# HGRN intra-chunk scores: one 128-column matmul against four 32-column matmuls, gathered in a compact tile

## The chip, the cores and the metric

The kernel runs on one core of a Trainium2 chip. The metric is the device time of one execution in microseconds (us); the time of a version is the median of several executions. The profile is of one further execution, taken by the hardware profiler.

## What is computed

The reference is one layer of a streaming encoder for 256 tokens of width 2048: a half SwiGLU block, a mixer with two recurrent branches, a cross attention, a second half SwiGLU block and a final norm. All weights are float32. The change touches only one branch of the mixer, the HGRN2 recurrence. Per head (8 heads, 128 key features, 128 value features) it is

```
S_t = diag(f_t) S_{t-1} + (1 - f_t) outer v_t,   o_t = S_t^T q_t
```

The reference works in chunks. The part that matters here is the score of a query token t against an earlier key token s, each feature decayed by the product of the forget gates between them:

```python
k = 1.0 - f
rel = b[:, :, :, None, :] - b[:, :, None, :, :]        # b: running sum of log f
decay = jnp.where(tri, jnp.exp(jnp.minimum(rel, 0.0)), 0.0)
scores = jnp.einsum('bhtk,bhsk,bhtsk->bhts', qc, kc, decay)
o_intra = jnp.einsum('bhts,bhsv->bhtv', scores, vc)
```

## The kernel before, in words

**The bulk of the kernel** is streamed weight products. A weight tile of 128x2048 float32 is fetched by a DMA on SP's queue, split by ScalarE (ACT, L120) into a high part in the reduced format fp32r and by VectorE (DVE, L121) into the rest, and multiplied by TensorE (PE) in three terms (`three` L446 to L452, `product` L224 to L245, `rows_product` L247 to L255). `weights` (L165) keeps two tiles prepared ahead of the one in use.

**The middle part** is a list of *units* (L876 to L901). A unit is one weight tile's product with the handling of its result: f, q, v, g for the HGRN branch in two halves of four heads, then the inputs of the other branch, then the gates. Beside them runs a list of *side jobs*, Python generators: `hgrn(0)`, `hgrn(1)`, `lru(0)`, `lru(1)`, `branch_a`. After each unit that does not return True, `pump(2)` (L658) advances the first side job by two steps; a step that ends in `yield True` ends the pump at once. `tc.issue_after(done["product"])` (L661) places what a side step issues on PE behind the unit's product. The framework orders the instructions of every engine at build time by their place in the program and its own model of when operands are ready; each engine then runs its list strictly in order.

**The HGRN job** (`hgrn`, L737 to L828) makes the score matrix of the 128 tokens of each of 2 groups x 4 heads, eight matrices in one SBUF tile `S` (128 partitions = key token, three times 512 columns; the third part holds the scores between the two groups). It works over levels n = 1, 2, 4, 8, 16, 32, 64 (`LEVELS`, L24): at level n a block of 2n tokens takes the scores of its second half's queries against its first half's keys, with q and k already decayed up to the block's middle. Ahead of the levels comes the diagonal (token against itself).

- Diagonal (L745 to L752): eight float32 matmuls with 128 key tokens as weight columns and 128 query tokens as moving columns, in two PSUM banks; DVE multiplies each bank by the identity into `S`.
- Levels 1 to 16 (L771 to L784): eight matmuls with 128 weight columns and the 64 queries that are in second halves; DVE multiplies the bank by a mask of 64 columns into a tile `part` (128x512), and in the next step adds `part` into the second halves' columns of `S`.
- Levels 32 and 64 (L759 to L770): for each block a matmul of its own, with n weight columns and n moving columns, placed at the block's partitions of the bank; ACT copies the blocks to `S` (L768).
- After each level DVE multiplies q and k by the block totals (L788), and makes the next totals (L793).
- The matrices then multiply the values (L807, L808), the result is normed and gated.

A float32 matmul stands in the trace as two records on PE and two weight loads on PEld.

`t1` (L90) hands out tiles of 128x256 float32 from a pool of eight, which the units use for the steps between accumulator and result (`summed`, L261).

Of the kernel before, what the change touches and what calls it, by code (L numbers as in the profile page):

```python
# [8 lines left out]
F32 = mybir.dt.float32  # L9
F32R = mybir.dt.float32r  # L10
ACT = mybir.ActivationFunctionType
ALU = mybir.AluOpType

P = 128
# [9 lines left out]
LEVELS = [1, 2, 4, 8, 16, 32, 64]  # L24
# [5 lines left out]
for _name, _n in [  # L30
    ("ffn1_norm", 16), ("mix_norm", 16), ("xattn_norm", 16), ("mem_norm", 16),
    ("ffn2_norm", 16), ("hgrn_norm", 8), ("lb0", 8), ("lb1", 8), ("lam", 8), ("conv_w", 32),
    ("conv_b", 8), ("ba", 8), ("bx", 8),
    ("ident", P), ("masks", 64 * 5),
]:
    VEC[_name] = (_at, _n)
    _at += _n
# [24 lines left out]
def block_kernel(ctx: ExitStack, tc: tile.TileContext, xT, xin, memT, vec, gfin, bgate, lruw, wu1, wd1, win, wv,  # L62
                 wg, wab, wout, wq, wk, wvm, wo, wu2, wd2, out_):
    nc = tc.nc
    pe, dve, act, sp = nc.tensor, nc.vector, nc.scalar, nc.sync
# [11 lines left out]
    scoped = {}  # L77
# [9 lines left out]
    def slot(dt=F32, name="slot"):  # L87
        return slots.tile([P, 1024], dt, name=name, tag="slot")

    def t1(name="t1"):  # L90
        return scoped["tmp"].tile([P, T], F32, name=name, tag="t1")

    def bank(name="acc"):
        return psum.tile([P, 512], F32, name=name, tag="acc")
# [6 lines left out]
    def col(name, i=0, n=1):  # L101
        a = VEC[name][0] + i
        return vt[:, a:a + n]
# [10 lines left out]
    ident = col("ident", 0, P)  # L114
# [551 lines left out]
    def heads(t):  # L666
        return t.rearrange("p (h t) -> p h t", h=4)
# [65 lines left out]


    Y = {}

    def hgrn(hf):  # L737
        q, f = Q[hf], F[hf]
        kk = slot(name="k")
        dve.tensor_scalar(out=kk, in0=f, scalar1=-1.0, scalar2=1.0, op0=ALU.mult, op1=ALU.add)  # L740
        yield True
        S = scoped["scores"].tile([P, 3 * 512], F32, name="S", tag="S")
        Sv = S.rearrange("p (g h t) -> p g h t", g=3, h=4)
        qv, kv = heads(q), heads(kk)
        for g in range(2):  # L745
            acc = bank()
            for h in range(4):
                pe.matmul(acc[:, h * P:(h + 1) * P], kv[:, h, g * P:(g + 1) * P], qv[:, h, g * P:(g + 1) * P],
                          start=True, stop=True)
            dve.tensor_tensor(out=Sv[:, g], in0=acc.rearrange("p (h t) -> p h t", h=4),  # L750
                              in1=ident[:, None, :].broadcast_to([P, 4, P]), op=ALU.mult)
            yield  # L752
        dve.tensor_tensor(out=q, in0=q, in1=f, op=ALU.mult)
        yield True
        tots = slot(name="tots")
        tot, at = f, 0
        for li, n in enumerate(LEVELS):
            acc = bank()
            if n >= 32:  # L759
                for g in range(2):  # L760
                    for h in range(4):
                        i = g * 4 + h
                        for a in range(0, P, 2 * n):
                            s = g * P + a
                            pe.matmul(acc[a:a + n, i * n:(i + 1) * n], kv[:, h, s:s + n], qv[:, h, s + n:s + 2 * n],
                                      start=True, stop=True)
                for a in range(0, P, 2 * n):
                    act.activation(S[a:a + n, :1024].rearrange("p (i t) -> p i t", t=P)[:, :, a + n:a + 2 * n],  # L768
                                   acc[a:a + n, :8 * n].rearrange("p (i n) -> p i n", n=n), ACT.Copy)
                yield  # L770
            for g in range(2 if n < 32 else 0):  # L771
                for h in range(4):
                    i = g * 4 + h
                    r = qv[:, h, g * P:(g + 1) * P].rearrange("p (j two n) -> p j two n", two=2, n=n)[:, :, 1]
                    pe.matmul(acc[:, i * 64:(i + 1) * 64], kv[:, h, g * P:(g + 1) * P], r, start=True, stop=True)  # L775
            if n < 32:
                part = scoped["tmp2"].tile([P, 512], F32, name="part", tag="part")
                dve.tensor_tensor(out=part.rearrange("p (i t) -> p i t", i=8),
                                  in0=acc.rearrange("p (i t) -> p i t", i=8),
                                  in1=col("masks", li * 64, 64)[:, None, :].broadcast_to([P, 8, 64]), op=ALU.mult)  # L780
                yield
                to = S[:, :1024].rearrange("p (i two n) -> p i two n", two=2, n=n)[:, :, 1]
                dve.tensor_tensor(out=to, in0=to, in1=part.rearrange("p (i n) -> p i n", n=n), op=ALU.add)
                yield  # L784
            pairs = tot.rearrange("p (j two) -> p j two", two=2)
            for t, side_of, by in ((q, 1, 0), (kk, 0, 1)):
                o = t.rearrange("p (j two n) -> p j two n", two=2, n=n)[:, :, side_of]
                dve.tensor_tensor(out=o, in0=o, in1=pairs[:, :, by:by + 1].broadcast_to([P, 512 // n, n]), op=ALU.mult)  # L788
                yield by == 1
            if n < 64:  # L790
                new = tots[:, at:at + 512 // n]
                at += 512 // n
                dve.tensor_tensor(out=new, in0=pairs[:, :, 0], in1=pairs[:, :, 1], op=ALU.mult)  # L793
                tot = new
        acc = bank()
        for h in range(4):
            pe.matmul(acc[:, h * P:(h + 1) * P], kv[:, h, :P], qv[:, h, P:], start=True, stop=True)
        act.activation(S[:, 1024:], acc, ACT.Copy)
        yield True
        y = Y["a", hf] = slot(name="ya")  # L800
        for pair in range(2):
            os, squares = [], []
            for z in range(2):
                h = pair * 2 + z
                c = (hf * 4 + h) * P
                o = bank()
                pe.matmul(o[:, :T], v[0][:, c:c + P], Sv[:, ::2, h, :], start=True, stop=False)  # L807
                pe.matmul(o[:, P:T], v[1][:, c:c + P], Sv[:, 1, h, :], start=False, stop=True)  # L808
                os.append(o)
                s = t1("osq")  # L810
                act.activation(s, o[:, :T], ACT.Square)
                squares.append(s)
            yield True
            ss = bank()
            for z in range(2):
                pe.matmul(ss[:, z * T:(z + 1) * T], ones, squares[z], start=True, stop=True)
            std = scoped["tmp2"].tile([P, 512], F32, name="ostd", tag="part")
            act.activation(std, ss, ACT.Sqrt, bias=eps, scale=1.0 / P)
            yield
            for z in range(2):  # L820
                h = pair * 2 + z
                o = heads(y)[:, h]
                r = std[:, z * T:(z + 1) * T]
                dve.reciprocal(out=r, in_=r)
                dve.tensor_tensor(out=o, in0=os[z][:, :T], in1=r, op=ALU.mult)
                dve.scalar_tensor_tensor(out=o, in0=o, scalar=col("hgrn_norm", hf * 4 + h), in1=heads(G[hf])[:, h],
                                         op0=ALU.mult, op1=ALU.mult)
                yield  # L828


    def lru(hf):
# [38 lines left out]
        yield  # L870
        y = Y["b", hf] = slot(name="yb")
        act.activation(GB[hf], GB[hf], ACT.Gelu_apprx_tanh)
# [20 lines left out]
    def branch_a():  # L893
        for h in range(8):
            ys.add(heads(Y["a", h // 4])[:, h % 4])
            yield
# [7 lines left out]
    for h in range(8):  # L904
        ys.add(heads(Y["b", h // 4])[:, h % 4])
    merged = Operands()
# [47 lines left out]
    for m in range(KT):  # L954
        acc = product(xs3.tiles, weights("q", m), late)
# [12 lines left out]
    for m in range(KT):  # L968
        acc = product(ms.tiles, weights("k", m))
# [38 lines left out]
    for g in range(4):  # L1008
# [4 lines left out]
        for t in range(2):  # L1013
            s = slot(F32R, "vs")
# [8 lines left out]
    for h in range(HEADS):  # L1023
        for j in range(4):
            acc = bank()
            for t in range(2):
                ps = probs[h][:, t * 512:(t + 1) * 512]
                s = vs[h, t]
# [50 lines left out]
def _layout(inputs):  # L1079
    import numpy as np  # L1080

    a = {k: np.asarray(v) for k, v in inputs.items()}
# [31 lines left out]
    def put(name, t):  # L1114
        at, n = VEC[name]
        vec[:, at:at + n] = t
# [6 lines left out]
    put("bx", vector(a["lru_bx"][0]))  # L1123
    put("lam", vector(a["lru_lambda"][0]))
    put("ident", np.eye(P, dtype=np.float32))
    s, t = np.arange(P)[:, None], np.arange(64)[None, :]
    put("masks", np.concatenate([(s // n == 2 * (t // n)) for n in LEVELS[:5]], axis=1).astype(np.float32))

    w = a["w_in"][0]
    win = columns(np.concatenate([w[:, :2048], w[:, 3072:6144]], axis=1))  # L1130
# [38 lines left out]
```

## Time and profile before

| what | value |
|---|---|
| median of 3 executions | 2468.77 us (2468.11 to 2469.32) |
| the profiled execution, its own time | 2467.42 us |
| its span in the profile | 2465.3 us |
| PE busy | 2446.9 us, 99% of the span |
| DVE busy | 1896.5 us, 77% |
| ACT busy | 1393.1 us, 57% |
| HGRN job of the first half of the heads | from 810.9 us to 949 us |
| HGRN job of the second half | from 937.8 us to 1088 us |
| diagonal matmuls, records on PE | 32 (16 matmuls) |
| level 1 to 16 matmuls, records on PE | 160 (80 matmuls) |
| granted TensorE clock | 0.999 |

Busy time is time in which an engine had at least one instruction in flight. A PE record's duration is longer than the interval at which PE starts records, since matmuls are pipelined; what a group of matmuls costs is read from the intervals between starts. The chain of waits is the work that ended last, followed back from the end of the execution; the length of a piece in it is the time it holds the end back.

### The profile page before, as it was taken

How to read it: one execution, taken by the hardware profiler on the slowest of the kernel's cores; microseconds unless marked ns; L12 is line 12 of the kernel's file. 1: busy time of each engine (PE TensorE's matmuls, PEld its weight loads, DVE VectorE, ACT ScalarE, POOL GpSimd, SP SyncE). 2: the span in 40 equal slices, each digit the busy share in tenths (PEclk: the TensorE clock that was granted, in tenths of full speed). 3: DMA queues.
4: the chain of work that ended last, by engine and by line, in shares of the span. 5: the costliest groups of instructions: out<-in, count | busy, mean ns of one | idle time of the engine just before them, and what ended most of it. 6: DMA issues, size and time to landing. Idle time of an engine off the chain costs nothing.

```text
span 2465.3 us, 29124 instructions
## 1 busy us (share of the span) xinstructions
PE 2446.9 (99%) x11674; PEld 2044.5 (83%) x11674; DVE 1896.5 (77%) x2016; ACT 1393.1 (57%) x1387; POOL 28.1 (1%) x36
## 2 busy tenths in 40 slices
PE   9999999999999999999999999999999999999998
PEld 7787888888888888888888888888888788888887
DVE  7989999999865757567665676556689899999995
ACT  8566666666564444358434554455555566666664
POOL 0000000000000000000000000000000000000000
PEclk9999999999999999999999999999999999999999
DMA  7567777777755455554655565554555777777774
GB/s 292 191 219 228 239 237 236 234 233 236 237 176 194 163 171 176 170 185 174 216 182 194 196 208 184 175 172 157 182 196 177 234 239 239 238 234 235 234 238 153
DMA packets 75303, 509.71 MB, mean 207 GB/s; under 512 B 8352, under 2 KB 8608, under 8 KB 15264
## 3 DMA queue, kind: packets, MB, share of 16 engines
q1 hardware_dynamic: 69840, 473.17, 56.0%
q0 software_dynamic: 4608, 33.56, 6.6%
q8 instruction: 91, 1.49, 0.2%
q10 hardware_dynamic: 720, 1.13, 0.1%
q14 instruction: 44, 0.36, 0.0%
HBM read 472.17 MB, written 2.10 MB: 192 GB/s over the span
## 4 chain that ended last, share of the span: by engine, by line
PE 92%; DVE 3%; ACT 2%; DMA 2%; issue 1%; SPq 0%; ACTq 0%; DVEq 0%
PE acc L452 16%; PE acc L449 16%; PE acc L450 16%; PE acc L231 11%; PE acc L252 8%; PE acc L253 8%; PE acc L255 8%; PE acc L235 5%; ACT h L120 1%; DMA raw<-wu 1%; DVE l L121 1%; PE acc L775 1%; PE acc L488 1%; PE acc L389 1%; DMA l<-raw 0%
## 5 line engine op out<-in xcount | busy, mean ns | idle before, releaser
L121 DVE TENSOR_TENSOR l<-raw,h 128x2048 fp32r<-128x2048 f32 (+2 forms) x420 | 874.8, 2085 | 334.7 <-ACT h L120 331.2
L120 ACT ACTIVATE h<-raw 128x2048 fp32r<-128x2048 f32 (+2 forms) x420 | 734.6, 1752 | 557.8 <-PE acc L253 227.1
L449 PE MATMUL acc<-h,xh 128*128 128x512 f32 x1280 | 500.3, 391 | 6.8 <-ACT h L120 6.7
L450 PE MATMUL acc<-h,xl 128*128 128x512 f32 x1280 | 497.7, 389 | 0.0
L120 ACT ACTIVATE h<-td 128x1024 fp32r<-128x1024 f32 x224 | 235.8, 1055 | 241.5 <-DVE td L213 103.5
L121 DVE TENSOR_TENSOR tl<-td,h 128x1024 fp32r<-128x1024 f32 x224 | 273.1, 1222 | 83.5 <-ACT h L120 54.5
L252 PE MATMUL acc<-h,ops 128*128 128x512 f32 x832 | 326.9, 393 | 0.0
L253 PE MATMUL acc<-h,ops 128*128 128x512 f32 x832 | 324.4, 390 | 0.0
L449 PEld LDWEIGHTS acc<-h,xh 128*128 128x128 f32 x1280 | 240.2, 188 | 61.7 <-ACT h L120 11.1
L450 PEld LDWEIGHTS acc<-h,xl 128*128 128x128 f32 x1280 | 240.3, 188 | 49.2
L231 PE MATMUL acc<-ops,h 128*128 128x512 f32 x1152 | 277.8, 393 | 0.3
L449 PE MATMUL acc<-h,hidop 128*128 128x512 f32 x704 | 275.8, 392 | 0.0
L450 PE MATMUL acc<-h,hidop 128*128 128x512 f32 x704 | 274.4, 390 | 0.0
L231 PEld LDWEIGHTS acc<-ops,h 128*128 128x128 f32 x1152 | 211.9, 188 | 42.6 <-DVE ops L292 0.9
L452 PE MATMUL acc<-l,xh 128*128 128x512 f32 x832 | 217.7, 389 | 0.0
L255 PE MATMUL acc<-l,ops 128*128 128x512 f32 x832 | 205.8, 389 | 0.0
L452 PE MATMUL acc<-l,hidop 128*128 128x512 f32 x704 | 188.3, 389 | 0.0
L452 PEld LDWEIGHTS acc<-l,xh 128*128 128x128 f32 x832 | 156.0, 188 | 32.7 <-DVE l L121 0.3
L255 PEld LDWEIGHTS acc<-l,ops 128*128 128x128 f32 x832 | 156.2, 188 | 32.4
L252 PEld LDWEIGHTS acc<-h,ops 128*128 128x128 f32 x832 | 156.3, 188 | 32.2
L253 PEld LDWEIGHTS acc<-h,ops 128*128 128x128 f32 x832 | 156.3, 188 | 31.6
L452 PEld LDWEIGHTS acc<-l,hidop 128*128 128x128 f32 x704 | 132.1, 188 | 27.6
(218 smaller groups left out, 2391.1 us busy)
## 6 DMA issues: line engine op xcount, KB each, us to landing
raw<-wu SPq DMA_DIRECT2D x172, 1024.0 KB, 5.2
raw<-wd SPq DMA_DIRECT2D x88, 1024.0 KB, 4.9
raw<-win SPq DMA_DIRECT2D x40, 1024.0 KB, 4.8
l<-raw POOLq DMA_DIRECT2D x32, 1024.0 KB, 11.0
raw<-wg SPq DMA_DIRECT2D x32, 1024.0 KB, 4.8
raw<-wab SPq DMA_DIRECT2D x16, 1024.0 KB, 4.9
raw<-wout SPq DMA_DIRECT2D x16, 1024.0 KB, 4.8
raw<-wq SPq DMA_DIRECT2D x16, 1024.0 KB, 4.8
```

The lines of the kernel that those rows point to most:

```text
L120: done["high"] = act.activation(h, raw, ACT.Copy).ins
L121: dve.tensor_tensor(out=l, in0=raw, in1=h.bitcast(F32), op=ALU.subtract)
L231: pe.matmul(acc, h[:, k * P:(k + 1) * P], xs[k], start=k == 0, stop=False)
L235: done["product"] = pe.matmul(acc[:, :T], l[:, k * P:(k + 1) * P], xs[k][:, :T], start=False, stop=k == KT - 1).ins
L252: pe.matmul(accs[t], x[:, t * P:][:, :P], h[j], start=first and j == 0, stop=False)
L253: pe.matmul(accs[t], x[:, T + t * P:][:, :P], h[j], start=False, stop=False)
L255: done["product"] = pe.matmul(accs[t], x[:, t * P:][:, :P], l[j], start=False, stop=last and j == 3).ins
L389: pe.transpose(accs[m // 2][:, m % 2 * T + t * P:][:, :P], tile[:, t * 512 + m * P:][:, :P], ident)
L449: pe.matmul(acc, ah, bh, start=start, stop=False)
L450: pe.matmul(acc, al, bh, start=False, stop=False)
L452: pe.matmul(acc, ah, bl, start=False, stop=stop)
L488: pe.transpose(acc[:, z * T + t * P:][:, :P], hid[t][:, (2 * y + z) * P:][:, :P], ident)
```

## The change

For the diagonal and the levels 1 to 16, the scores only ever lie within blocks of 32 tokens. The change computes only those blocks. A new inner function `within(n, out)` runs 32 matmuls in place of eight: for each of the eight matrices and each of the four blocks of 32 tokens one, with 32 weight columns (the block's keys) and 32 moving columns (diagonal, n = 0) or 16 (the block's second-half queries). The four blocks of a matrix go to the four quarters of the bank's partitions, and the same columns. DVE multiplies the bank's first 256 or 128 columns by a mask.

The results are gathered in a compact tile `own` of 128x256 (partition = key token, 8 matrices x 32 query tokens), taken from the pool of `t1`; `part` is now 128x128 from the same pool. After level 16, four ACT copies (32 partitions x 256 columns each) bring the blocks from `own` to the diagonal blocks of `S`.

`S` is allocated once for both halves and its first 1024 columns are zeroed by one DVE memset ahead of the units. The diagonal is now one step of the side job and not two. The mask table shrinks from 320 to 112 columns. Levels 32 and 64 and all after them are as before.

```diff
-    ("ident", P), ("masks", 64 * 5),
+    ("ident", P), ("masks", 32 + 16 * 5),
...
+    S = scoped["scores"].tile([P, 3 * 512], F32, name="S", tag="S")
+    dve.memset(S[:, :1024], 0.0)
 
     def hgrn(hf):
...
-        S = scoped["scores"].tile([P, 3 * 512], F32, name="S", tag="S")
         Sv = S.rearrange("p (g h t) -> p g h t", g=3, h=4)
         qv, kv = heads(q), heads(kk)
-        for g in range(2):
-            acc = bank()
-            for h in range(4):
-                pe.matmul(acc[:, h * P:(h + 1) * P], kv[:, h, g * P:(g + 1) * P], qv[:, h, g * P:(g + 1) * P],
-                          start=True, stop=True)
-            dve.tensor_tensor(out=Sv[:, g], in0=acc.rearrange("p (h t) -> p h t", h=4),
-                              in1=ident[:, None, :].broadcast_to([P, 4, P]), op=ALU.mult)
-            yield
+        own = t1("own")
+
+        def within(n, out):
+
+            acc, wide = bank(), 16 if n else 32
+            for i in range(8):
+                for b in range(4):
+                    at = i // 4 * P + b * 32
+                    r = qv[:, i % 4, at:at + 32]
+                    if n:
+                        r = r.rearrange("p (j two n) -> p j two n", two=2, n=n)[:, :, 1]
+                    pe.matmul(acc[b * 32:(b + 1) * 32, i * wide:(i + 1) * wide], kv[:, i % 4, at:at + 32], r,
+                              start=True, stop=True)
+            m = col("masks", 32 + 16 * (n.bit_length() - 1), 16) if n else col("masks", 0, 32)
+            dve.tensor_tensor(out=out.rearrange("p (i t) -> p i t", i=8),
+                              in0=acc[:, :8 * wide].rearrange("p (i t) -> p i t", i=8),
+                              in1=m[:, None, :].broadcast_to([P, 8, wide]), op=ALU.mult)
+
+        within(0, own)
+        yield
         dve.tensor_tensor(out=q, in0=q, in1=f, op=ALU.mult)
         yield True
...
-            for g in range(2 if n < 32 else 0):
-                for h in range(4):
-                    i = g * 4 + h
-                    r = qv[:, h, g * P:(g + 1) * P].rearrange("p (j two n) -> p j two n", two=2, n=n)[:, :, 1]
-                    pe.matmul(acc[:, i * 64:(i + 1) * 64], kv[:, h, g * P:(g + 1) * P], r, start=True, stop=True)
-            if n < 32:
-                part = scoped["tmp2"].tile([P, 512], F32, name="part", tag="part")
-                dve.tensor_tensor(out=part.rearrange("p (i t) -> p i t", i=8),
-                                  in0=acc.rearrange("p (i t) -> p i t", i=8),
-                                  in1=col("masks", li * 64, 64)[:, None, :].broadcast_to([P, 8, 64]), op=ALU.mult)
+            else:
+                part = t1("part")[:, :P]
+                within(n, part)
                 yield
-                to = S[:, :1024].rearrange("p (i two n) -> p i two n", two=2, n=n)[:, :, 1]
+                to = own.rearrange("p (i two n) -> p i two n", two=2, n=n)[:, :, 1]
                 dve.tensor_tensor(out=to, in0=to, in1=part.rearrange("p (i n) -> p i n", n=n), op=ALU.add)
+                if n == 16:
+                    for a in range(0, P, 32):
+                        act.activation(S[a:a + 32, :1024].rearrange("p (i t) -> p i t", t=P)[:, :, a:a + 32],
+                                       own[a:a + 32].rearrange("p (i t) -> p i t", t=32), ACT.Copy)
                 yield
```

More of the change, by code (lines that the diff above doesn't have):

```diff
@@ L756, in hgrn @@
         tot, at = f, 0
-        for li, n in enumerate(LEVELS):
-            acc = bank()
+        for n in LEVELS:
             if n >= 32:
+                acc = bank()
                 for g in range(2):
@@ L1125, in _layout @@
     put("ident", np.eye(P, dtype=np.float32))
-    s, t = np.arange(P)[:, None], np.arange(64)[None, :]
-    put("masks", np.concatenate([(s // n == 2 * (t // n)) for n in LEVELS[:5]], axis=1).astype(np.float32))
+    s, t = np.arange(P)[:, None] % 32, np.arange(32)[None, :]
+    masks = [s == t] + [s // n == 2 * (t[:, :16] // n) for n in LEVELS[:5]]
+    put("masks", np.concatenate(masks, axis=1).astype(np.float32))
     w = a["w_in"][0]
```

## The prediction, made before the changed kernel ran

> **What bounds the kernel now.** I read the page's busy times and its chain first, then the stretches in which the HGRN jobs run, then the chain of waits inside them.
>
> ```profile
> PE 2446.9 (99%) x11674; PEld 2044.5 (83%) x11674; DVE 1896.5 (77%) x2016; ACT 1393.1 (57%) x1387; POOL 28.1 (1%) x36
> ...
> PE 92%; DVE 3%; ACT 2%; DMA 2%; issue 1%; SPq 0%; ACTq 0%; DVEq 0%
> ```
> ```profile
> core 0: us, PE busy (x) PEld busy (x) DVE busy (x) ACT busy (x) POOL busy (x), PEclk, DMA share, GB/s
> 810.00:950.00 140.00, 140.00 (x848) 123.63 (x847) 95.56 (x118) 60.74 (x65) 0.00 (x0) 1.00 0.49 166
> 950.00:1090.00 140.00, 140.00 (x781) 120.39 (x780) 89.32 (x97) 62.44 (x55) 0.00 (x0) 1.00 0.51 177
> ```
>
> PE carries 92% of the chain of the whole execution, but that is an average. The two stretches of the HGRN jobs say it for the place of the change: PE is busy for 140.00 of 140 us in each, at a granted clock of 1.00, while DVE works 95.56 and 89.32 us and ACT about 61 us. Here PE time alone counts, and all of it counts; DVE time saved buys nothing by itself. What a side step costs on PE is read in the chain, from its own piece and from the stretch of the product behind it:
>
> ```profile
> 812.33 1.79 PE acc L748 x16
> 814.12 3.67 PE acc L231 x16
> 817.79 1.91 PE acc L235 x16
> 819.70 3.65 PE acc L231 x16
> ...
> 825.27 1.74 PE acc L775 x16
> 827.00 3.73 PE acc L231 x16
> ...
> 889.48 0.63 PE acc L765 x32
> 890.11 3.85 PE acc L231 x16
> ```
>
> The high products (L231) take 3.65 us where no side step stands ahead of them. So the eight diagonal matmuls cost 1.79 + 0.02 = 1.81 us, eight matmuls of a level from 1 to 16 cost 1.74 + 0.08 = 1.82 us, and the level-32 group costs 0.63 + 0.20 = 0.83 us. That last group, 16 matmuls with 32 weight columns and 32 moving columns, is the nearest thing in this trace to what the change adds.
>
> **The change on PE: what goes.**
>
> ```profile
> L748 PE MATMUL acc<-silu,k x32: 272/275/275, 812.2 to 954.1; 128*128 128x128 f32 x32
> ```
> ```profile
> L775 PE MATMUL acc<-silu,k x160: 217/275/275, 825.1 to 1018.5; 128*128 128x64 f32 x160
> ```
>
> Sixteen records make a piece of the chain, so the diagonal has 2 pieces and the levels 10. They cost 2 x 1.81 + 10 x 1.82 = 21.8 us, all of it on the path. Note that 128 moving columns cost no more than 64: the step is set by its 128 weight columns, not by what is streamed.
>
> **What comes.** Twelve pieces of 32 matmuls, 64 records each. How fast these run decides the case. The level-32 row has two column groups (its outputs begin at partitions 0 and 64), the level-64 row one group of 64 columns. Counting the records begun up to a moment, in short stretches of these two pieces:
>
> ```profile
> core 0: us, PE busy (x) PEld busy (x), PEclk, DMA share, GB/s
> 889.30:889.42 0.12, 0.01 (x2) 0.01 (x2) 1.00 1.44 609
> 889.30:889.58 0.28, 0.17 (x10) 0.17 (x12) 1.00 1.03 439
> 889.30:889.90 0.60, 0.49 (x30) 0.49 (x32) 1.00 1.04 440
> 901.30:901.42 0.12, 0.05 (x1) 0.05 (x1) 1.00 1.61 683
> 901.30:901.64 0.34, 0.27 (x4) 0.27 (x5) 1.00 1.02 434
> 901.30:902.22 0.92, 0.85 (x14) 0.86 (x15) 1.00 1.00 426
> ```
>
> One group of 64 columns begins 10 records in 0.58 us, 58 ns each. Half as many columns in one group should take about half, 29 to 32 ns. But level 32 begins 20 records in 0.32 us, 16 ns each, and has two in flight before the first 64-column record is followed by a second. So the two groups run side by side, each with a record every 32 ns. The rest of the 0.83 us is paid once per piece: 32 records x 16 ns = 0.51 us leaves 0.32 us around it, of which 0.20 us is the late product behind.
>
> In the changed kernel each of the four groups gets eight matmuls, 16 records, in every piece. That is exactly what each of the two groups has at level 32. If four groups run side by side as two do, a piece lasts 16 x 32 ns = 0.51 us and costs 0.83 us again. From below, nothing in these rows makes a group faster than 32 ns (fewer moving columns did not help above); from above, all four in turn would take 64 x 32 ns = 2.0 us, which the two-group row speaks against. I take 0.83 us: twelve pieces are 10.0 us, and the sum on PE is 10.0 - 21.8 = **-11.8 us**.
>
> The Trainium skill ("TensorE: Matmul & The Clock Gate", Part 3: Packing small matmuls) gives a speed-up of 2.38 for three column groups with long streams, four fifths of ideal; as an estimate from it, four groups would reach 3.2, a piece would cost 0.32 + 2.0 / 3.2 = 0.95 us, and the sum would be -10.4 us. Our two-group row shows no such loss, so I keep my value.
>
> **DVE, ACT and the queues.**
>
> ```profile
> L783 DVE TENSOR_TENSOR S<-S,part 128x512 f32<-128x512 f32 x10 | 6.9, 687 | 0.0
> ...
> L778 DVE TENSOR_TENSOR part<-acc,vt 128x512 f32<-128x512 f32 x10 | 6.8, 683 | 0.0
> ...
> L750 DVE TENSOR_TENSOR S<-acc,vt 128x512 f32<-128x512 f32 x4 | 2.7, 683 | 0.0
> ...
> L768 ACT ACTIVATE S<-acc 32x256 f32<-32x256 f32 x4 | 1.5, 376 | 0.8 <-PE acc L765 0.8
> ```
> ```profile
> L266 DVE TENSOR_TENSOR sum<-acc,lo 128x256 f32<-128x256 f32 x72 | 29.9, 418 | 0.0
> ...
> L432 DVE TENSOR_TENSOR xs<-xg 128x128 f32<-128x128 f32 x40 | 9.6, 286 | 0.0
> ```
>
> DVE loses 16.4 us (6.9 + 6.8 + 2.7) and gains 2 x 0.42 + 20 x 0.29 = 6.6 us. ACT gains 8 x 0.376 = 3.0 us. I cost both at nothing: PE is the cover, with 45 and 80 us of slack per stretch. If that cover were gone, DVE's 9.8 us would come off the path too, so the sign is with the change.
>
> The four ACT copies after level 16 add a wait: they need DVE's last addition, and queued behind them on ACT are the next weight tile's high part (L120) and the unit's own copy out of PSUM (L264). PE waits for the first only two tiles later, since two are prepared ahead; at 5.6 us a unit (3.65 + 1.91) this hides the 1.5 us of the copies and a few us of waiting. The price if it did not is some 2 us in each half. The diagonal being one step and not two, the level-1 matmuls come one unit sooner after q times f:
>
> ```profile
> 816.84 1.22 DVE L753 TENSOR_TENSOR silu<-silu,f 128x1024 f32<-128x1024 f32 x1
> ```
>
> DVE was through with it at 818.06, after two masks of 0.68 us; the earlier level-1 matmuls would stand at 812.33 + 0.83 + 5.56 = 818.7, and one mask less is to be done. I cost it at nothing. `own` holds one of the eight tiles of `t1` for some ten units; a unit needs two or three. Nothing is late by that.
>
> The memset of `S` is new, 1024 columns, on DVE, at the passage from the first SwiGLU block.
>
> ```profile
> L106 DVE MEMSET ones<- x1: 165/165/165, 0.8 to 0.8; 128x128 f32 x1
> ```
> ```profile
> L862 DVE MEMSET m<- x2: 62/62/62, 1121.6 to 1157.9; 128x4 f32 x2
> ```
> ```profile
> 708.76 0.69 DVE L558 SCALAR_TENSOR_TENSOR x<-acc,x 128x512 f32<-128x512 f32 x1
> 710.95 0.69 DVE L558 SCALAR_TENSOR_TENSOR x<-acc,x 128x512 f32<-128x512 f32 x1 [1.50 <-PE acc L452]
> 712.10 2.29 DVE L121 TENSOR_TENSOR l<-raw,h 128x2048 fp32r<-128x2048 f32 x1 [0.46 <-ACT h L120]
> ```
>
> From 4 to 128 columns a memset grows by 103 ns, so 1024 take about 0.91 us. DVE has an idle 1.50 us there, waiting for PE, in which it fits; put just ahead of the L121 at 712.10 it would hold the next norm's operands and cost up to 0.9 us. I take 0 and keep 0.9 for the range. On SP's queue the one load of the masks gets shorter; nothing waits for it.
>
> **Sum.** The profiled execution took 2467.42 us (2465.3 of span, 2.1 around it); -11.8 gives 2455.6. The median of the three runs is 1.35 us above that execution, so a median should stand at **2457.0 us**, 0.5% faster. About 0.2%, 4.9 us, is what a measurement of this kernel can tell from no change.
>
> **The rivals.**
>
> *Only two groups at a time*, or equally a floor of 16 ns between any two records: the rows show two groups, never four, and the two are not neighbours. A piece then costs 0.32 + 64 x 16 ns = 1.34 us, twelve 16.1, the sum -5.7 us: **2463.1 us**. This is also the form in which the change would not do what it says. Against it speaks only that nothing in the two-group row looks saturated. The Trainium skill ("TensorEngine Tiling (Array Packing)", Instruction Overhead) speaks against the change more strongly: every matmul carries some 60 cycles, and no factor is to be had from a dimension that is small already. As an estimate, at the 2.4 GHz of its TensorE page, 25 ns for each of 64 records make 1.6 us, a piece 1.9 us, and the time would be 2470. Our row of 16 ns a record is under that floor.
>
> *PE's sequencer cannot feed the burst.* A piece is now 128 instructions (64 weight loads, 64 matmuls); the longest quick burst so far was level 32 with 64.
>
> ```profile
> L765 PEldq EVENT_SEMAPHORE  x3: 51/51/51, 887.0 to 1037.2; - x3
> ```
> ```profile
> 887.41 2.07 PE L235 MATMUL acc<-ops,l 128*128 128x256 f32 x16
> 889.41 0.70 PE L765 MATMUL acc<-silu,k 128*32 128x32 f32 x32
> ```
>
> The sequencer met the wait of level 32 at 887.0, about 18 matmuls and 18 loads ahead of the engine. If it holds 36 instructions, 28 of the 64 came in during the 0.51 us of the burst without slowing it, so it delivers one in at most 18 ns; then a piece lasts at most 92 x 18 ns = 1.66 us and costs 1.98, the sum is +1.9 us, **2470.7 us**, the worst of "no change". If it holds 64, the whole level-32 burst was queued beforehand and says nothing of the rate; all that bounds it is L235, 32 instructions in 1.91 us, 60 ns each. Then 64 instructions come at that rate: 0.32 + 64 x r, which is slower than before from r = 23 ns, slower by 0.2% from 30 ns, and at 60 ns +28 us. At 40 ns, between these, it is **2481 us**: the case on the other side. For it speaks that no burst this long exists in the trace; against it the 36.
>
> **How the numbers follow.** Four groups side by side, or three: 0.60, with a range of its own of 2455.5 to 2459.5 (three side by side cost 0.32 + 0.67 = 0.99 us a piece, -9.9 us). Two at a time: 0.18, around 2463, two thirds of it beyond the 0.2%. Sequencer, not slower: 0.14, 2464 to 2471. Sequencer, slower: 0.08. So faster 0.60 + 0.12 = 0.72, same 0.06 + 0.14 = 0.20, slower 0.08. The range reaches from 2455.0 through the second case and the first part of the third, with the memset's 0.9 us: to 2466.0.
>
> **What would show it.** In the profile after, the pieces of the new matmuls in the chain should be 0.6 to 0.7 us for 64 records, with 3.85 us of L231 behind them, and four records should begin in the first 0.04 us; 1.1 us with records in pairs would be the second case; a quick first part of the piece and a slower rest would be the sequencer. PE should stay busy without a gap from 810 to 1080, the second half's job should end some 20 us earlier, and DVE's busy time should fall by about 9 us. I am wrong in kind if PE shows idle time in that stretch, or at the passage around 710 to 717.

## The result and the profile after

The changed kernel takes 2454.99 us (median of 4 runs, 2454.05 to 2455.41), the kernel before 2468.53 us in the same comparison: ratio 0.9948, 95% interval 0.9935 to 0.9960. Timed again on another occasion it took 2455.91 us against 2467.49, ratio 0.9952 (0.9939 to 0.9964). So the change is worth 11.6 to 13.5 us. The forecast was 11.8 us and 2457.0 us; the first median stands on the lower edge of the range of 2455.0 to 2466.0 (0.01 us under it, where executions of one kernel scatter by more than 1 us).

The profiled execution has a span of 2452.3 us, 13.0 less than before. First the busy times, then the two stretches of the HGRN jobs:

```profile
PE 2436.5 (99%) x12250; PEld 2032.2 (83%) x12250; DVE 1887.3 (77%) x2015; ACT 1402.5 (57%) x1399; POOL 28.1 (1%) x36
```
```profile
810.00:950.00 140.00, 140.00 (x1289) 121.69 (x1288) 95.48 (x120) 65.61 (x72) 0.00 (x0) 1.00 0.49 173
950.00:1090.00 140.00, 140.00 (x966) 118.09 (x965) 86.55 (x100) 74.58 (x72) 0.00 (x0) 1.00 0.53 184
```

PE is still busy without a gap at a clock of 1.00, so the gain is PE work that is gone and not a wait. The chain of waits gives the new price of a piece (L757 is the matmul in `within`, L778 is level 32, which did not change):

```profile
811.84 0.69 PE acc L757 x50
...
818.30 0.67 PE acc L757 x52
818.96 3.85 PE acc L231 x16
...
877.83 0.63 PE acc L778 x32
878.46 3.85 PE acc L231 x16
```

A piece with all its 64 records (the chain skips the records that ran beside another) takes 0.67 us, the diagonal's 0.69, and the product behind is 0.20 us late as after level 32: 0.87 to 0.89 us, where it was 1.82. How the records begin, counted in stretches of the level-1 piece:

```profile
core 0: us, PE busy (x) PEld busy (x), PEclk, DMA share, GB/s
818.10:818.26 0.16, 0.03 (x4) 0.03 (x5) 1.00 0.84 358
818.10:818.34 0.24, 0.11 (x12) 0.11 (x16) 1.00 0.97 410
818.10:818.50 0.40, 0.27 (x32) 0.27 (x34) 1.00 0.59 246
818.10:818.60 0.50, 0.37 (x44) 0.37 (x46) 1.00 0.48 197
818.10:818.76 0.66, 0.53 (x62) 0.53 (x64) 1.00 0.45 174
```

Four records begin almost together (7 ns apart). From 818.34 to 818.50 there are 20 in 0.16 us, 8 ns each: four in the time that one group needs for one. From 818.60 to 818.76 it is 18 in 0.16 us, slightly slower; the doubled run below follows this second pace further.

**Where the 13 us are.** The middle part can be timed apart from the two SwiGLU blocks: from the first product on PE that reads the mixer's input (L231) to the first of the second SwiGLU block (L449). The kernel before, then the changed one:

```profile
710.75 0.61 PE L231 MATMUL acc<-ops,h 128*128 128x512 f32 x2
...
1759.21 0.39 PE L449 MATMUL acc<-h,xh 128*128 128x512 f32 x1
```
```profile
710.29 0.61 PE L231 MATMUL acc<-ops,h 128*128 128x512 f32 x2
...
1747.77 0.39 PE L449 MATMUL acc<-h,xh 128*128 128x512 f32 x1
```

The middle takes 1048.46 us before and 1037.48 after, 10.98 us less. The other 2.0 us are outside it, 0.46 ahead and 1.56 behind, where PE's order did not change. The second profile of the changed kernel has the same middle, 1037.47 us, and a span of 2455.1. What differs between the kernel before and the first profile of the changed one is mainly how long PE waited for split weights in the SwiGLU blocks. PE's waits of the kernel before, of the changed one, and of the changed one again:

```profile
PE acc L449 <- ACT h L120: 6.7, 8, 1.7
```
```profile
PE acc L449 <- ACT h L120: 4.2, 5, 1.7
```
```profile
PE acc L449 <- ACT h L120: 6.6, 7, 1.7
```

The changed kernel waited 2.5 us less in its first profile and as long as the kernel before in its second. The second profile has one more cause, a stretch in the first SwiGLU block in which the granted clock was 0.50:

```profile
79.00:82.40 3.40, 3.40 (x9) 2.64 (x10) 3.18 (x2) 2.50 (x3) 0.00 (x0) 0.50 0.81 299
```

There a matmul holds the chain for 0.43 us where it holds it for 0.23 at a clock of 1.00. That makes some 1.5 us of the 2.8 us by which the two spans of the changed kernel differ.

So the 2 us are scatter between executions. The middle repeats within 0.1 us where whole executions scatter by more than 1 us, and I use it below beside the medians.

**The other steps.** The memset and the ACT copies of the changed kernel, and the product of q and f on DVE:

```profile
L792 ACT ACTIVATE S<-own x8: 399/414/417, 869.5 to 1000.8; 32x256 f32<-32x256 f32 x8
...
L737 DVE MEMSET S<- x1: 912/912/912, 658.7 to 658.7; 128x1024 f32 x1
```
```profile
815.17 1.22 DVE L766 TENSOR_TENSOR silu<-silu,f 128x1024 f32<-128x1024 f32 x1
```

The memset takes the 0.91 us of the estimate, but was put 50 us sooner than I looked for it, at 658.7, while DVE waited for PE. The product of q and f is through at 816.39, ahead of the matmuls at 818.2 that need it. DVE's busy time fell by 9.2 us (forecast 9.8).

### The profile page after: what moved, and what is told of

It reads as the page before. It is cut to its first block, busy times and chain, and to the rows that moved or that the text cites. A ratio compares the mean times of both kernels' runs of the same rounds, so it can differ in the third digit from the quotient of the medians.

```text
span 2452.3 us, 30292 instructions
## 1 busy us (share of the span) xinstructions
PE 2436.5 (99%) x12250; PEld 2032.2 (83%) x12250; DVE 1887.3 (77%) x2015; ACT 1402.5 (57%) x1399; POOL 28.1 (1%) x36
## 4 chain that ended last, share of the span: by engine, by line
PE 92%; DMA 3%; DVE 3%; issue 1%; ACT 1%; SPq 0%; ACTq 0%; POOLq 0%; DVEq 0%
PE acc L452 16%; PE acc L449 16%; PE acc L450 16%; PE acc L231 11%; PE acc L252 8%; PE acc L253 8%; PE acc L255 8%; PE acc L235 5%; DMA raw<-wu 2%; DVE l L121 1%; DMA l<-raw 1%; PE acc L488 1%; ACT h L120 1%; PE acc L389 1%; DVE tl L121 0%
## 5 line engine op out<-in xcount | busy, mean ns | idle before, releaser
L449 PE MATMUL acc<-h,xh 128*128 128x512 f32 x1280 | 500.3, 391 | 4.3 <-ACT h L120 4.2
L252 PE MATMUL acc<-h,ops 128*128 128x512 f32 x832 | 326.9, 393 | 0.0
L449 PEld LDWEIGHTS acc<-h,xh 128*128 128x128 f32 x1280 | 240.3, 188 | 59.0 <-ACT h L120 8.4
L231 PE MATMUL acc<-ops,h 128*128 128x512 f32 x1152 | 277.9, 393 | 0.3
L449 PE MATMUL acc<-h,hidop 128*128 128x512 f32 x704 | 275.9, 392 | 0.0
L231 PEld LDWEIGHTS acc<-ops,h 128*128 128x128 f32 x1152 | 211.9, 188 | 42.8 <-DVE ops L292 0.9
L252 PEld LDWEIGHTS acc<-h,ops 128*128 128x128 f32 x832 | 156.3, 188 | 32.3
```

What stands on the lines that cost most here:

```text
L231: pe.matmul(acc, h[:, k * P:(k + 1) * P], xs[k], start=k == 0, stop=False)
L252: pe.matmul(accs[t], x[:, t * P:][:, :P], h[j], start=first and j == 0, stop=False)
L449: pe.matmul(acc, ah, bh, start=start, stop=False)
```

## The experiments

Times are medians; "middle" is the stretch defined above, 1048.46 us before and 1037.48 us in the changed kernel, read in the same two rows of each profile.

### The changed kernel again

> The changed kernel itself, timed in more rounds, to see how much of the 13.5 us is the change. Theory: the twelve pieces explain 12 x (1.82 - 0.87) = 11.4 us, and the other 2 us are waits for weights in the two SwiGLU blocks, which differ from one execution to the next; then the medians should lie 11 to 14 us apart, and the PE waits of the SwiGLU blocks in this profile need not repeat those of the first one. Rival: the 2 us belong to the change (the memset, the new order of DVE and ACT); then the same SwiGLU waits are short again and 13.5 us repeats.

2455.91 us against 2467.49; middle 1037.47 us. The SwiGLU waits were back at 6.6 us, and the half-clock stretch near 80 us came on top; the same short waits did not repeat, and neither did the 13.5 us, so the rival falls. The theory holds, except that the waits are not the whole of the scatter. 11.6 us is the better figure of the two medians, and the 10.98 us of the middle is free of what happens in the SwiGLU blocks.

### The same matmuls, one column group after the other

```diff
-            for i in range(8):
-                for b in range(4):
+            for b in range(4):
+                for i in range(8):
```

> The changed kernel with the same 32 matmuls in another order: all eight of the first block of 32 tokens, then all eight of the second, and so on, so that matmuls that follow one another go to the same column group. Theory (groups work side by side, a group takes 32 ns for a record): 64 x 32 ns = 2.05 us and a piece costs about 2.37 us in place of 0.87, 12 x 1.5 = +18 us over the changed kernel, 2473 us, slower than the kernel before. Rival (matmuls with 32 columns are cheap by themselves, 8 ns a record whatever the group): no change, 2455 us.

2469.08 us, 13.2 us more than the changed kernel, and ratio 1.0006 (0.9997 to 1.0015) to the kernel before; middle 1051.46 us. The chain, and records begun in a level-1 piece:

```profile
819.72 1.83 PE acc L757 x64
821.55 3.85 PE acc L231 x16
```
```profile
819.60:819.72 0.12, 0.07 (x2) 0.07 (x3) 1.00 0.00 0
819.60:820.04 0.44, 0.39 (x12) 0.39 (x13) 1.00 0.00 0
```

From 819.72 to 820.04 ten records begin in 0.32 us: 32 ns each, the pace of one group. A piece costs 1.83 + 0.20 = 2.03 us, more than the 1.82 of eight wide matmuls. Against the 2.37 expected, 64 x 32 ns = 2.05 us was too long by the overlap where one group hands over to the next: in the trace some records begin there only 5 to 6 ns after the one ahead. The change of order alone takes the whole gain away. So narrow matmuls by themselves gain nothing; the gain is in the order that goes round the four groups. A second profile of the same kernel:

> The same kernel as the one with the groups in turn, one look only, for a second profile of it. Theory: again 2473 us, with pieces of about 2.2 us in the chain.

2470.19 us, pieces of 1.83 and 1.84 us again, where 2.2 had been written down; the middle is again 1051.5 us.

### Two groups at a time

```diff
-            for i in range(8):
-                for b in range(4):
+            for i, b in [(i, c + z) for c in (0, 2) for i in range(8) for z in range(2)]:
+                if True:
```

> The changed kernel with the same matmuls ordered so that two column groups alternate (the first and second for all eight matrices, then the third and fourth). Theory (side by side): 64 records at 16 ns, 1.01 us, a piece costs 1.37 us, 12 x 0.5 = +6 us over the changed kernel, 2461 us. Rival (PE's sequencer or a floor between any two records sets the pace, not the groups): no change, 2455 us. A second rival, that neighbouring groups disturb each other where the first and third of level 32 do not: more than +6 us.

2459.43 us, ratio 0.9969 (0.9958 to 0.9980) to the kernel before, 3.5 us over the changed kernel; middle 1041.88 us, 4.4 over it.

```profile
817.87 1.03 PE acc L757 x62
818.90 3.85 PE acc L231 x16
```
```profile
817.70:818.00 0.30, 0.20 (x12) 0.20 (x14) 1.00 0.01 0
817.70:818.19 0.49, 0.39 (x24) 0.40 (x26) 1.00 0.01 0
```

Twelve records in 0.19 us are 16 ns each, the pace of level 32, with neighbouring groups. So neighbours do not disturb each other, and it is the number of groups that sets the pace: 32, 16 and 8 ns for one, two and four. A piece costs 1.23 us, 0.14 below the expectation, for the most part again by the overlap at the hand-over.

### The kernel before, with S allocated once

```diff
     Y = {}
+    S = scoped["scores"].tile([P, 3 * 512], F32, name="S", tag="S")
+    dve.memset(S[:, :1024], 0.0)
...
-        S = scoped["scores"].tile([P, 3 * 512], F32, name="S", tag="S")
```

> The kernel before with nothing of the change but the tile S allocated once and zeroed by the memset. Theory (only the PE pieces matter): within 0.2% of the kernel before, 2468.5 us give or take 1.5. Rival (the 2 us that the pieces do not explain come from the other allocation and order): about 2466.5 us.

2467.66 us, ratio 1.0001 (0.9992 to 1.0009); middle 1048.44 us. The allocation and the memset change nothing that these runs can tell.

### Each burst issued twice, and four times

```diff
-            for i in range(8):
+            for i in [*range(8), *range(8)]:
```

> The changed kernel with each piece's 32 matmuls issued twice over into the same places (the same scores result). A piece is then 128 records, 256 instructions. Theory (side by side, and the sequencer keeps up): the second 64 records cost 64 x 8 to 8.3 ns = 0.51 to 0.53 us, 12 x 0.52 = +6.2 us over the changed kernel, 2461 us, and the rest of a piece, 0.36 us, is paid once. Rival (the sequencer feeds the array more slowly once what it holds is used up, at up to 18 ns an instruction): the second 64 records, 128 instructions, cost up to 2.3 us, +28 us, 2483 us.

2464.84 us, 8.9 us over the changed kernel. The chain of the doubled run:

```profile
831.98 1.20 PE acc L757 x84
833.18 0.43 PE acc L231
833.61 1.97 issue
835.58 1.55 PE acc L231 x6
```

A piece takes 1.20 us, 0.53 more for 64 more records: 8.3 ns each. So the slightly slower pace of the second half of a burst goes on without a break; 8.3 ns is 4% above the 8.0 of its first half. In the traces the pattern changes at about the 35th record of a burst, in the changed, the doubled and the fourfold run alike: ahead of it the records come in rounds of four, behind it in pairs about 16.7 ns apart. What sets this second pace was not tested. Twelve pieces make 6.4 us. Most of the rest is one gap of 1.97 us in which PE waits for nothing that the profile shows, right behind a burst. To see whether it belongs to the burst (`4 * [*range(8)]` in the same line):

> The changed kernel with each piece's 32 matmuls issued four times over into the same places (the scores stay as they are). A piece is 256 records, 512 instructions. The doubled run showed the second 64 records at 8.3 ns each and one PE gap of 1.97 us behind a burst that waited for nothing the profile shows. Theory (the gap is tied to long bursts: the instructions of the next product are not there in time): records still at 8.3 ns, 12 x 3 x 0.53 = +19 us over the changed kernel, and several gaps of about 2 us behind bursts, together 2475 to 2490 us. Rival (the one gap was chance): +19 us, 2475 us, and no such gap.

2518.82 us, ratio 1.0208 (1.0194 to 1.0222). The chain around one burst, and PE's waits from 805 to 1100 us:

```profile
813.90 2.04 PE acc L757 x131
815.95 2.22 issue
818.17 0.45 PE acc L757 x27
```
```profile
PE acc L757 <- issue: 23.4, 11, 2.6
PE acc L231 <- issue: 2.7, 1, 2.7
```

Eleven gaps lie inside the bursts and not behind them as expected, ten of 1.9 to 2.6 us and one of 0.8. One more, of 2.7 us, lies behind a burst. Together they are 26 us. Eleven of the twelve bursts met one, one of them two. The time is some 29 us beyond the range that was expected. The middle is 1097.75 us, 60.3 over the changed kernel; the records explain 19 of these and the gaps 26. The expectation had no term for the clock. In six stretches of the middle, 27 us together, the granted clock fell to 0.50, as in this one, which begins 0.9 us after the end of a gap of 2.52 us:

```profile
860.00:867.58 7.58, 5.05 (x276) 1.00 0.63 203
867.58:870.99 3.41, 3.41 (x9) 0.50 0.42 173
```

At half the clock these stretches cost some 12 us (an estimate: half of their time, without the gap that lies in one of them), and about 3 us stay open. The gaps come with the length of the burst. The page counts 91 packets on the instruction queue before, 96 in the changed kernel, 102 doubled and 114 fourfold:

```profile
q8 instruction: 91, 1.49, 0.2%
```
```profile
q8 instruction: 114, 1.87, 0.3%
```

That is 16 KB a packet. That PE runs out of instructions until the next packet lands fits these rows; it is argued from them, not shown, since no run removes the gap and keeps the length.

### DVE's work put back

```diff
+            pad = scoped["tmp2"].tile([P, 512], F32, name="pad", tag="part")
+            for _ in range(2):
+                dve.tensor_tensor(out=pad, in0=kk[:, :512], in1=kk[:, 512:], op=ALU.mult)
```

> The changed kernel with two extra DVE products of 128x512 in each of the twelve steps, whose result nobody reads: 24 x 0.685 = 16.4 us of DVE work, more than the change took away. Theory (DVE has slack in this part): no change, 2455 us. Rival (the smaller work of DVE gave part of the gain, the 2 us that the pieces do not explain): 2457 us or more, with PE idle between 810 and 1080.

2455.92 us, the same as the changed kernel's 2455.91; middle 1037.60 us. The two stretches:

```profile
810.00:950.00 140.00, 140.00 (x1289) 121.67 (x1288) 105.09 (x136) 65.70 (x72) 0.00 (x0) 1.00 0.48 167
950.00:1090.00 140.00, 140.00 (x965) 118.03 (x965) 92.71 (x109) 73.73 (x72) 0.00 (x0) 1.00 0.54 191
```

DVE works 15.8 us more in these two stretches than in the changed kernel, and PE has no gap. The compact tile's smaller DVE work is worth nothing here.

### Both halves in one piece

A generator takes `hgrn(0)` and `hgrn(1)` step by step together, each with its own `S`; the pool of `t1` has six tiles, the 128x512 scratch one buffer.

```diff
+    def both():
+        for one, two in zip(hgrn(0), hgrn(1)):
+            assert one == two
+            yield one
...
-        units += [lambda hf=hf: side.append(hgrn(hf)) or True]
+    units += [lambda: side.append(both()) or True]
```

> The changed kernel with the HGRN jobs of both halves of the heads run in step, so that each piece on PE holds the matmuls of both halves: twelve pieces become six. (Two tiles S; to make room, six tiles in the pool of t1 in place of eight, one in place of two in that of the 128x512 scratch.) Theory (what stands around a piece, 0.36 us, is paid once per piece): 6 x 0.36 = 2.2 us less for these pieces and some 0.6 us less for levels 32 and 64, 2452 us. Rival (the steps are twice as heavy for DVE and ACT, and scratch is short): PE waits at the next piece, 2456 us or more.

2458.34 us; middle 1041.11 us, 3.6 over the changed kernel. The joint pieces took 1.25 us, less than two pieces apart, but the chain shows that the time was lost in another place:

```profile
1019.93 2.29 DVE l L121
1022.23 3.27 DVE ostd L836 x2
...
1025.83 0.80 PE acc L252
1026.63 0.43 PE acc L253
```
```profile
1022.00:1026.00 4.00, 0.55 (x4) 0.35 (x3) 4.00 (x5) 3.71 (x7) 0.00 (x0) 0.82 0.71 219
1026.00:1030.00 4.00, 4.00 (x10) 3.12 (x11) 4.00 (x10) 1.12 (x2) 0.00 (x0) 0.50 0.42 174
1030.00:1031.36 1.36, 1.36 (x5) 1.08 (x4) 1.36 (x5) 0.00 (x0) 0.00 (x0) 0.50 0.00 0
```

Two reciprocals of the norm, late behind a weight's split on DVE, hold PE for 3.5 us, and afterwards PE runs at a granted clock of 0.50 until 1031.36, for 5.5 us: a matmul holds the chain for 0.43 us where it held it for 0.23. So only the levels were put together, and the norms left apart:

```diff
+        one, two = hgrn(0), hgrn(1)
+        for _ in range(30):
+            next(one)
+            yield next(two)
+        yield from one
+        yield from two
```

> As the run with both halves in step, but only up to the scores; the products with the values and the norms follow one half after the other, as in the changed kernel. Theory: the PE gap of that run came from the doubled norm steps on DVE (four reciprocals of 1.74 us in a step); without it the shared pieces pay: about 0.29 us for each of six pairs, 0.2 to 0.3 us for each of the pairs of levels 32, 64 and the last, 2.4 us less on PE than in the changed kernel, 2453.5 us. Rival: a pair of levels in step is too much for DVE as well, or the later start of the jobs moves them into busier units; then PE shows a gap again and the time is 2456 us or more.

2452.85 us, ratio 0.9941 (0.9927 to 0.9954); middle 1035.28 us, 2.2 us less than the changed kernel, where 2.4 were expected. The joint level-1 piece:

```profile
907.92 1.25 PE acc L759 x101
909.17 3.85 PE acc L231 x16
```

A joint piece costs 1.45 us where two cost 1.74. PE has no gap in this part, so it was the doubled norm steps that had made the gap. This is the fastest version. Its lead over the changed kernel is 3 us by the medians, which were taken on different occasions, and 2.2 us by the middle.

## Why the prediction was right, step by step

Two lines of the chain of the kernel before bear on the price of what went. They show a level piece with the other form of product behind it:

```profile
851.15 1.73 PE acc L775 x16
852.88 0.28 PE acc L252
```

- *PE time alone counts in these stretches*: right. DVE's work put back changed nothing, and no gap appeared on PE.
- *The diagonal and levels 1 to 16 cost 21.8 us in 12 pieces of 1.81 to 1.82*: right within 0.2 us. With the measured prices of the new pieces the sum gives the middle of three kernels: 12 x (0.87 - 1.82) = -11.4 against -10.98 measured, 12 x (2.03 - 1.82) = +2.5 against +3.0 in turn, 12 x (1.23 - 1.82) = -7.1 against -6.6 in pairs. Each measured value is 0.4 to 0.5 us slower than its sum. About half of this is the price of what went. The 1.82 us was read from one level-1 piece with the product of L231 behind it and carried to all ten. Five of the ten cost 1.78 to 1.79, four of them ahead of the other form of product: its first matmul (L252) holds the chain for 0.28 to 0.29 us where one without a piece ahead holds it for 0.23, so it adds only 0.05 to 0.06 us to the 1.73. Piece by piece, 21.6 us went and not 21.8. The other 0.2 to 0.3 us stay open.
- *Four groups run side by side as two do, a piece costs 0.83 us again*: right in the mechanism, shown by the runs in turn and in pairs. The size was off by 0.04 us for a level and 0.06 for the diagonal (0.87 and 0.89): the second half of a burst runs at 8.3 ns a record and not 8.0. By this term the sum was 0.5 us too good.
- *Two groups at a time, 1.34 us a piece* (the rival): this is not what the change does. When forced, it costs 1.23 us. The Trainium skill ("TensorEngine Tiling (Array Packing)", Instruction Overhead) gives some 60 cycles per matmul, 25 ns by the estimate in the prediction. That does not hold across column groups here: four groups begin a record every 8 ns. One group by itself, at 32 ns, is over that floor.
- The estimate from the Trainium skill's speed-up of three groups ("TensorE: Matmul & The Clock Gate", Part 3: Packing small matmuls), 0.95 us a piece, was too careful: the measured 0.87 is nearer to the ideal 0.83.
- *The sequencer cannot feed the burst* (the rival on the other side): not at this length. 128 instructions went through at 8.0 to 8.3 ns for a load and a matmul, where the rival allowed up to 18 ns for each instruction. But longer bursts do meet a limit: twice the length brought one gap of 2 us in twelve bursts, four times the length twelve gaps. The harm came in another form than the rival had it: stalls, not a much slower steady rate.
- *Memset hidden*: right, though in another idle time than the one named.
- *ACT gains 3.0 us*: too low. The copies took 8 x 0.414 = 3.3 us, but busy time rose by 9.4. The rest is mostly table loads (1.283 us each, 28 before and 32 after, 5.1 us), probably because jobs that come a unit sooner mix with other activations; that was not tested. It was hidden, as PE's 140 of 140 us show.
- *The signs*: right. PE has no gap from 810 to 1080 us nor at the passage around 710, and the norm's last matmul of the second half begins at 1057.8 us and not 1080.4, 22.6 us sooner where some 20 were forecast.
- *The sum and the level*: 11.8 forecast, 10.98 in the middle, 11.6 by the longer comparison. The two mis-sized terms explain the difference to the middle but for 0.1 us: 11.8 - 0.5 - 0.2 = 11.1. The first comparison's extra 2 us are scatter in the SwiGLU blocks and not part of the change. So it is partly luck that the forecast of 11.8 lies between the two measured differences: against the middle the sum is 0.8 us too large, and scatter added 0.6 to 2.5 us to the measured ones.

## What to carry to other kernels

A matmul whose useful output is block-diagonal can be cut into 32-column matmuls for the four quarters of the output's partitions. What it pays depends on the order of the instructions: by the middle, going round the four quarters won 11.0 us here, two quarters at a time 6.6, and quarter by quarter lost 3.0 against the uncut matmuls. Price such a change from the nearest burst in the trace, with the pace of one group, the number of groups and what stands around the burst (0.36 us here) as separate terms; and when PE is busy without a gap, leave DVE's savings out of the sum. Time the stretch that the change is in, between two fixed instructions, where whole executions scatter more than a term of the sum.

## What the runs showed of the hardware that was not expected

- Records of four column groups that take turns begin 8 ns apart on average, those of two groups 16 ns and those of one group 32 ns, with 32 or 16 moving columns alike.
- Long bursts of short matmuls meet gaps of 0.8 to 2.7 us, most of them about 2, in which PE waits for nothing shown: none in 12 bursts of 128 instructions, one in 12 of 256 (none in the six joint pieces of that length), twelve in 12 of 512.
- A PE gap can cost more than its own length, by the clock. In the run with both halves in step the granted clock fell to 0.50 some 2.2 us into a gap of 3.5 us and stayed there for 5.5 us after PE went on. The Trainium skill ("TensorE: Matmul & The Clock Gate", Part 1: The HAM clock gate) describes such a fall to half rate after a window of about 3.4 us idle. The half rate agrees; the idle time does not, since shorter gaps were followed by it too. In the fourfold run a clock of 0.50 began at the end of a gap of 1.9 to 2.6 us, or within 1.3 us behind it, six times. In the second profile of the changed kernel it fell at 79.0 us, 1.6 us after a gap of 1.7 us; in the first profile the same gap cost no clock. What decides it was not found.
